# Moving the sums of an output stage from GpSimd to VectorE in a fused decoder layer

## The chip, the cores and the metric

The kernel runs on one core of a Trainium2 chip. The time of a run is the device time in microseconds (us). The engines have names in the profile: PE is TensorE (its weight loads are PEld), DVE is VectorE, ACT is ScalarE, POOL is GpSimd, and SP starts transfers.

## What is computed

One decoder layer over 1024 tokens of width 1024, all in float32: a SwiGLU feed-forward, a mixer, a second feed-forward, and a last RMSNorm. Around each of the three there is a norm before it and a gated residual behind it.

```python
mod = jax.nn.silu(c) @ ada_w[l] + ada_b[l]
sh1, sc1, gt1, sh2, sc2, gt2, sh3, sc3, gt3 = jnp.split(mod, 9, axis=-1)
u = modulate(rmsnorm(h, norm1_w[l]), sh1, sc1)
h = h + 0.5 * gt1[:, None, :] * swiglu(u, ffn1_w_in[l], ffn1_w_out[l])
u = modulate(rmsnorm(h, norm2_w[l]), sh2, sc2)
...                                  # mixer: sparse attention and retention, merged into `mixed`
h = h + gt2[:, None, :] * (mixed @ w_out[l])
u = modulate(rmsnorm(h, norm3_w[l]), sh3, sc3)
h = h + 0.5 * gt3[:, None, :] * swiglu(u, ffn2_w_in[l], ffn2_w_out[l])
return rmsnorm(h, final_norm_w)
```

The three products that end in `h + ...` are the output products: two with a contraction of 2816 (the feed-forwards) and one with a contraction of 1024 (`mixed @ w_out`). They are what the change is about.

## The kernel before, in words

`h` is kept transposed in eight tiles `hT[d]` of 128 features by 1024 tokens; `hf` is the half of the tokens (512 each). Every float32 product is made of three products of a faster type: each operand is split into a high part (ScalarE, a rounding copy) and a low part (VectorE, the difference to the original), and TensorE adds high by high, high by low and low by high.

The output products run in `out_seven`. It uses a Strassen-Winograd scheme: a 2 by 2 block product is made of seven block products `q` instead of eight, at the price of sums of blocks before and after. The contraction is walked in chunks of pairs of row blocks, (4, 3, 4) pairs in the feed-forwards and one chunk of 4 pairs in the projection (`single`). For each chunk and each `q` there are four PSUM tiles `po[d]` and, for each pair `k`, twelve matmuls of 128x128 by 128x512.

- `ops(c, k, q)` makes the operands. For `q` of 5, 7 and 6 it sums blocks of the weights on the engine `left` (`s1`, `s3`, `s2`; L659, L663, L668) and blocks of the gated product on `right`, VectorE (L660, L665, L670). Then ScalarE copies the high parts (L678) and VectorE makes the low parts (L679) of two operands into a tile `wp`, of which there are four. After 2 or 6 it makes two more sums (L683 on VectorE, L685).
- `post` takes a finished `po[d]`: for `q` of 2, 3 and 4 the residual, on VectorE (`residual`, L789, which multiplies by the gate and adds to `hT`), and for the others a copy into an accumulator by ScalarE (L706). In the last chunk of a feed-forward a sum of two accumulators stands behind `q` = 1 (L708).
- `between` makes further sums of accumulators in the last chunk (L716 to L726), and one more residual. Before `q` with an accumulator, ScalarE copies the accumulator into `po` (L751).
- `squares` prepares the next norm: ScalarE squares a half tile of `hT` (L194 for the first of a half, L197 else, into a temporary of which there are two for each half), and a sum adds it to `sqacc` (L198). `rstd_cols` then reduces `sqacc` over partitions on TensorE (L207) and takes a root on ScalarE (L210) and a reciprocal on VectorE (L211).

In `finish` (the last norm) ScalarE and GpSimd scale `hT` (L1274, L1276), TensorE transposes (L1284), and VectorE and ScalarE write the output rows (L1290, L1288). GpSimd has other work of its own near these stages: the gated merge before the projection (L1241), and the low parts of one pair of weights of the second feed-forward (L261).

The order of the instructions on each engine isn't written out by hand: a planner puts them in order from the program's order and its own estimate of their times, with some parts marked as urgent. Each engine works through its queue in that order; an instruction that waits holds up those behind it.

Of the kernel before, what the change touches and what calls it, by code (L numbers as in the profile page):

```python
# [48 lines left out]
def f32(ap):  # L49
    return ap.bitcast(F32)  # L50


class Layer:
# [135 lines left out]
    def squares(self, d, hf, pool, state, i):  # L189
        nc = self.nc  # L190
        h = self.hT[d][:, hf * H2:(hf + 1) * H2]
        if hf not in state:
            state[hf] = pool.tile([P, H2], F32, name="sqacc", bufs=2)
            nc.scalar.activation(state[hf], h, AF.Square)  # L194
        else:
            q = self.tmp.tile([P, H2], F32, name="t2" if hf else "t1", bufs=2)
            nc.scalar.activation(q, h, AF.Square)  # L197
            (nc.vector if (i != 2 and d == 3 if hf else d > 3) else nc.gpsimd).tensor_add(state[hf], state[hf], q)  # L198

    def rstd_cols(self, hf, pool, sums, state):  # L200

# [393 lines left out]
    def out_seven(self, i, chunks, wsrc, gsrc, free, acc, state, then, have=None):  # L595
# [3 lines left out]
        nc = self.nc  # L599
        single = len(chunks) == 1  # L600
# [4 lines left out]
        chunks = prs  # L605
# [45 lines left out]
        def ops(c, k, q):  # L651

            g = lambda n: have[c, k, n][1]
            drop = lambda n: free.append(have.pop((c, k, n)))
            ren = lambda a, b: have.__setitem__((c, k, b), have.pop((c, k, a)))
            left = nc.vector if single and q == 7 else nc.gpsimd
            right = nc.vector
            if q == 5:
                left.tensor_add(g("s1"), g("b1"), g("b2"))  # L659
                right.tensor_sub(g("b11"), g("b12"), g("b11"))  # L660
                ren("b11", "t1")
            elif q == 7:
                left.tensor_sub(g("b1"), g("a1"), g("b1"))  # L663
                ren("b1", "s3")
                right.tensor_sub(g("b12"), g("b22"), g("b12"))  # L665
                ren("b12", "t3")
            elif q == 6:
                left.tensor_sub(g("s1"), g("s1"), g("a1"))  # L668
                ren("s1", "s2")
                right.tensor_sub(g("t1"), g("b22"), g("t1"))  # L670
                ren("t1", "t2")
                drop("a1")
            n = {1: ("a1", "b11"), 2: ("a2", "b21"), 3: ("s4", "b22"), 4: ("b2", "t4"), 5: ("s1", "t1"),
                 6: ("s2", "t2"), 7: ("s3", "t3")}[q]
            w = self.W.tile([P, 2, 2, H2], F32R, name="wp", bufs=self.wb)
            res = []
            for x in range(2):
                nc.scalar.copy(w[:, x, 0], g(n[x]))  # L678
                nc.vector.tensor_sub(w[:, x, 1], g(n[x]), f32(w[:, x, 0]))  # L679
                res.append((w[:, x, 0], w[:, x, 1]))  # L680
            done.append((c, k, q))
            if q in (2, 6) and (c, k, 8 - q) in done:
                right.tensor_sub(g("b21"), g("b21"), g("t2"))  # L683
                ren("b21", "t4")
                (nc.vector if single else left).tensor_sub(g("a2"), g("a2"), g("s2"))  # L685
                ren("a2", "s4")
                drop("s2")
                drop("t2")
            if q in (3, 4, 7):
                for x in n:  # L690
                    drop(x)
            return res

        def res(r, hf, d, x, end=False):
            self.residual(i, 4 * r + d, hf, x)
            if end:
                self.squares(4 * r + d, hf, self.normp, state, i)
# [3 lines left out]
        def post(q, d, p, c, last):  # L701
            A = {x: acc[x][d] for x in acc}
            if q in (2, 3, 4):
                res(q == 4, q == 3, d, p, last)
                return
            nc.scalar.copy(A[1 if q == 6 and single else q], p)  # L706
            if last and q == 1 and not single:
                nc.gpsimd.tensor_add(A[6], A[6], A[1])  # L708

        def between(q):  # L710

            for d in range(4):
                A = {x: acc[x][d] for x in acc}
                if single:
                    if q == 2:
                        nc.gpsimd.tensor_add(A[1], A[1], A[7])  # L716
                        nc.gpsimd.tensor_sub(A[7], A[5], A[7])
                    elif q == 6:
                        nc.gpsimd.tensor_add(A[5], A[5], A[1])
                        res(1, 1, d, A[5])  # L720
                        nc.gpsimd.tensor_add(A[7], A[7], A[1])
                elif q == 6:
                    nc.gpsimd.tensor_add(A[7], A[7], A[6])
                elif q == 4:
                    nc.gpsimd.tensor_add(A[6], A[6], A[5])
                    nc.gpsimd.tensor_add(A[7], A[7], A[5])  # L726
                    res(1, 1, d, A[7])

        fetch()
        for c, prs in enumerate(chunks):  # L730
            last = c == len(chunks) - 1
            m = len(prs)
            for j, q in enumerate((1, 2, 5, 7, 6, 4, 3) if not last else (1, 5, 7, 2, 6, 4, 3) if single else
# [18 lines left out]
                if last and (q == 2 if single else q == 4):  # L752
                    between(q)
# [6 lines left out]
                if q == 3 and last and m <= self.wb:  # L760
                    xs = [ops(c, k, q) for k in range(m)]
                    for d in range(4):
                        for k in range(m):
                            mm(d, k, *xs[k])
                        post(q, d, po[d], c, last)
                        next(then, None)
                        next(then, None)
                    continue
                for k in range(m):
                    x = ops(c, k, q)  # L770
                    fetch()
                    for d in range(4):
                        mm(d, k, *x)
                for d in range(4):
                    post(q, d, po[d], c, last)
                if last and q == 6:
                    between(q)
# [821 lines left out]
```

## Time and profile before

| | us |
|---|---|
| median of 3 runs | 2420.77 |
| lowest and highest | 2418.34, 2423.05 |
| the profiled execution | 2416.41 |
| its span, first to last instruction | 2414.6 |
| TensorE busy in it | 2268.8 |
| VectorE busy | 1814.4 |
| ScalarE busy | 1055.3 |
| GpSimd busy | 1220.1 |

The profile shows one execution. Its rows give for a group of instructions the engine, the line of the kernel, the operation, the tile written and the tiles read, their shape, and how many there are. Idle time before an instruction is put down to the instruction that ended it. Busy time of TensorE is modelled, since matmuls are pipelined; the count of matmuls is the safer number.

### The profile page before, as it was taken

What the parts mean: (1) busy time and instruction counts of PE and PEld (TensorE: products, weight loads), DVE (VectorE), ACT (ScalarE), POOL (GpSimd) and SP (SyncE); (2) the same over time, 40 slices, a digit from 0 to 9 for tenths busy, and PEclk for the clock granted to TensorE, in tenths of its full rate; (3) what the DMA queues carried; (4) which work ended last, traced back from release to release, by engine and by line L of the source; (5) the groups of instructions that cost most, each with busy time, mean ns of one, the idle gap of its engine ahead of it and who ended that gap; (6) DMA issues with size and microseconds to landing.
All of it is one profiled execution on the core that took longest, in us unless ns stands there. A gap on an engine that the chain in (4) does not pass through costs nothing.

```text
span 2414.6 us, 32683 instructions
## 1 busy us (share of the span) xinstructions
PE 2268.8 (94%) x11563; PEld 1903.5 (79%) x11563; DVE 1814.4 (75%) x2742; ACT 1055.3 (44%) x1904; POOL 1220.1 (51%) x900
## 2 busy tenths in 40 slices
PE   7799999999997999999997999999889999999997
PEld 5578888878876899887876889877668888887886
DVE  7888888578999855677667887759885555558987
ACT  5432222235764322123347776725432222225675
POOL 3856354544476544464315544456754444436447
PEclk9999999999998999999998999999889999999998
DMA  9135656263204344343552121460322222245301
GB/s 349 58 102 170 208 168 200 90 236 131 88 1 135 92 139 129 101 144 117 158 154 80 62 88 62 162 214 1 105 64 84 79 82 80 79 164 208 103 17 70
DMA packets 248888, 288.32 MB, mean 119 GB/s; under 512 B 14852, under 2 KB 169236, under 8 KB 248724
## 3 DMA queue, kind: packets, MB, share of 16 engines
q1 hardware_dynamic: 248608, 286.19, 37.2%
q8 instruction: 91, 1.49, 0.3%
q14 instruction: 73, 0.60, 0.1%
q10 hardware_dynamic: 116, 0.05, 0.0%
HBM read 216.45 MB, written 69.73 MB: 119 GB/s over the span
## 4 chain that ended last, share of the span: by engine, by line
PE 32%; DVE 9%; DMA 3%; ACT 3%; issue 2%; POOL 1%; SPq 0%; DVEq 0%; ACTq 0%; POOLq 0%
PE po L281 17%; DVE wp L679 3%; PE s L758 3%; PE po L758 3%; PE ot L1173 2%; PE pt L1159 2%; PE s L281 2%; PE s L1071 1%; DMA tn<-d_gab 1%; DVE hT L789 1%; PE s L1070 1%; DMA hT<-d_h 1%; PE pt L862 1%; PE ot L1170 0%; PE po L495 0%
## 5 line engine op out<-in xcount | busy, mean ns | idle before, releaser
L281 PE MATMUL po<-u0h,wp 128*128 128x512 f32 x944 | 305.3, 395 | 7.3 <-DVE gates L998 4.9
L758 PE MATMUL po<-wp 128*128 128x512 f32 x1128 | 271.8, 397 | 17.1 <-DVE wp L679 16.3
L281 PE MATMUL po<-u1h,wp 128*128 128x512 f32 x880 | 282.0, 391 | 3.5 <-DVE bias L544 2.2
L758 PEld LDWEIGHTS po<-wp 128*128 128x128 f32 x1128 | 214.6, 192 | 70.5 <-DVE wp L679 24.7
L758 PE MATMUL s<-wp 128*128 128x512 f32 x1056 | 252.5, 395 | 15.6 <-DVE wp L679 15.0
L758 PEld LDWEIGHTS s<-wp 128*128 128x128 f32 x1056 | 199.8, 190 | 62.8 <-DVE wp L679 20.5
L334 ACT CAST wp<-S 128x1024 fp32r<-128x1024 f32 x98 | 103.0, 1051 | 307.1 <-PE po L281 303.1
L281 PEld LDWEIGHTS po<-u0h,wp 128*128 128x128 f32 x944 | 179.5, 190 | 46.1 <-DVE gates L998 5.1
L463 POOL TENSOR_TENSOR t<-t,t 128x512 f32<-128x512 f32 x38 | 56.3, 1482 | 303.0 <-DVE t L407 193.7
L281 PEld LDWEIGHTS po<-u1h,wp 128*128 128x128 f32 x880 | 165.1, 188 | 40.3 <-DVE bias L544 2.6
L281 PE MATMUL po<-u0l,wp 128*128 128x512 f32 x472 | 186.1, 394 | 0.0
L281 PE MATMUL po<-u1l,wp 128*128 128x512 f32 x440 | 172.5, 392 | 2.5 <-DVE u1l L243 2.5
L335 DVE TENSOR_TENSOR wp<-S,wp 128x1024 fp32r<-128x1024 f32 x98 | 158.7, 1619 | 16.1 <-ACT wp L334 15.9
L334 ACT CAST wp<-raw 128x1024 fp32r<-128x1024 f32 x98 | 82.0, 837 | 185.7 <-PE po L281 174.1
L341 POOL TENSOR_TENSOR S<-raw 128x512 f32<-128x512 f32 x49 | 68.9, 1406 | 155.1 <-DMA raw<-w_in 47.6
L281 PE MATMUL po<-t2h,wp 128*128 128x512 f32 x392 | 132.2, 397 | 3.0 <-ACT t2h L300 3.0
L281 PE MATMUL po<-t4h,wp 128*128 128x512 f32 x392 | 131.5, 396 | 1.1 <-DVE tn L399 1.1
L281 PE MATMUL po<-t3h,wp 128*128 128x512 f32 x392 | 132.0, 397 | 0.2 <-DVE t L395 0.2
L335 DVE TENSOR_TENSOR wp<-raw,wp 128x1024 fp32r<-128x1024 f32 x98 | 113.0, 1154 | 12.0 <-ACT wp L334 11.8
L395 DVE TENSOR_TENSOR t<-tn,po 128x512 f32<-128x512 f32 x57 | 39.1, 685 | 110.3 <-issue 78.5
L1163 DVE TENSOR_TENSOR pl<-pt,ph 128x512 fp32r<-128x512 f32 (+2 forms) x160 | 97.0, 619 | 13.8 <-ACT ph L1162 13.0
L281 PEld LDWEIGHTS po<-u0l,wp 128*128 128x128 f32 x472 | 90.0, 191 | 18.3
(467 smaller groups left out, 6195.2 us busy)
## 6 DMA issues: line engine op xcount, KB each, us to landing
raw<-ffn_w_in SPq DMA_DIRECT2D x88, 512.0 KB, 4.7
raw<-ada_w SPq DMA_DIRECT2D x56, 512.0 KB, 4.5
raw<-w_in SPq DMA_DIRECT2D x40, 512.0 KB, 4.1
d_g<-t SPq DMA_DIRECT2D x50, 256.0 KB, 2.0
d_h<-hT SPq DMA_DIRECT2D x24, 512.0 KB, 4.7
hT<-d_h SPq DMA_DIRECT2D x48, 256.0 KB, 5.3
d_g<-tg SPq DMA_DIRECT2D x38, 256.0 KB, 2.0
fw<-ada_w SPq DMA_DIRECT2D x8, 1024.0 KB, 11.0
```

The source lines that it names most:

```text
L281: nc.tensor.matmul(ps, a, b, start=k == 0 and q == 0, stop=k == n - 1 and q == 2)
L334: nc.scalar.copy(w[:, 0], t)
L335: nc.vector.tensor_sub(w[:, 1], t, f32(w[:, 0]))
L341: nc.gpsimd.tensor_add(s[:, 0:4], b[:, 0:4], b[:, 4:8])
L395: nc.vector.tensor_add(c, u2, p)
L463: nc.gpsimd.tensor_mul(g, g, t)
L679: nc.vector.tensor_sub(w[:, x, 1], g(n[x]), f32(w[:, x, 0]))
L758: nc.tensor.matmul(po[d], l[:, e], r, start=k == 0 and z == 0 and not seeded, stop=k == m - 1 and z == 2, skip_group_check=seeded)
L789: self.nc.vector.scalar_tensor_tensor(h, po, self.ab[:, 3 * i + 2, d:d + 1], h, op0=ALU.mult, op1=ALU.add)
L1159: nc.tensor.transpose(pt[:, o + j * P:o + (j + 1) * P], a, self.ident)
L1163: nc.vector.tensor_sub(lo, pt[:, :n], f32(hi))
L1173: nc.tensor.matmul(ot, self.V2[kt // 4][:, kt % 4, b, g, :], x[:, o:o + 2 * P], start=first and m == 0, stop=last and m == 1)
```

## The change

All sums of the last chunk of the output products, and all sums of squares, are made on VectorE. In earlier chunks of the feed-forwards `left` stays GpSimd. In the projection the one chunk is also the last.

```diff
         else:
             q = self.tmp.tile([P, H2], F32, name="t2" if hf else "t1", bufs=2)
             nc.scalar.activation(q, h, AF.Square)
-            (nc.vector if (i != 2 and d == 3 if hf else d > 3) else nc.gpsimd).tensor_add(state[hf], state[hf], q)
+            nc.vector.tensor_add(state[hf], state[hf], q)
...
-            left = nc.vector if single and q == 7 else nc.gpsimd
+            left = nc.vector if c == len(chunks) - 1 else nc.gpsimd
...
-                (nc.vector if single else left).tensor_sub(g("a2"), g("a2"), g("s2"))
+                left.tensor_sub(g("a2"), g("a2"), g("s2"))
...
             if last and q == 1 and not single:
-                nc.gpsimd.tensor_add(A[6], A[6], A[1])
+                nc.vector.tensor_add(A[6], A[6], A[1])
...
                 if single:
                     if q == 2:
-                        nc.gpsimd.tensor_add(A[1], A[1], A[7])
-                        nc.gpsimd.tensor_sub(A[7], A[5], A[7])
+                        nc.vector.tensor_add(A[1], A[1], A[7])
+                        nc.vector.tensor_sub(A[7], A[5], A[7])
                     elif q == 6:
-                        nc.gpsimd.tensor_add(A[5], A[5], A[1])
+                        nc.vector.tensor_add(A[5], A[5], A[1])
                         res(1, 1, d, A[5])
-                        nc.gpsimd.tensor_add(A[7], A[7], A[1])
+                        nc.vector.tensor_add(A[7], A[7], A[1])
                 elif q == 6:
-                    nc.gpsimd.tensor_add(A[7], A[7], A[6])
+                    nc.vector.tensor_add(A[7], A[7], A[6])
                 elif q == 4:
-                    nc.gpsimd.tensor_add(A[6], A[6], A[5])
-                    nc.gpsimd.tensor_add(A[7], A[7], A[5])
+                    nc.vector.tensor_add(A[6], A[6], A[5])
+                    nc.vector.tensor_add(A[7], A[7], A[5])
                     res(1, 1, d, A[7])
```

## Rows read from the trace of the kernel before

**Rows 1.** The page, part 1: busy time, share of the span, instructions.
```profile
PE 2268.8 (94%) x11563; PEld 1903.5 (79%) x11563; DVE 1814.4 (75%) x2742; ACT 1055.3 (44%) x1904; POOL 1220.1 (51%) x900
```
**Rows 2.** Windows: stretch, length; busy us and instructions; granted clock, DMA share, GB/s.
```profile
580.00:632.00 52.00, 51.85 (x229) 42.64 (x228) 48.56 (x58) 35.50 (x66) 24.27 (x14) 1.00 0.26 82
655.40:689.60 34.20, 33.97 (x151) 27.80 (x150) 28.82 (x35) 26.59 (x51) 18.40 (x8) 1.00 0.00 1
689.60:731.20 41.60, 35.70 (x140) 27.23 (x138) 41.46 (x34) 24.58 (x44) 36.37 (x22) 0.92 0.00 0
1619.10:1640.40 21.30, 14.71 (x53) 10.09 (x51) 21.30 (x21) 9.41 (x17) 15.29 (x10) 0.92 0.00 1
1655.40:1706.80 51.40, 45.11 (x185) 34.96 (x183) 50.59 (x45) 30.96 (x54) 37.49 (x24) 0.97 0.10 41
2345.10:2390.70 45.60, 40.17 (x162) 31.64 (x160) 45.46 (x41) 28.62 (x51) 43.03 (x28) 0.93 0.00 1
```
**Rows 3.** Timeline, TensorE's weight loads: start, duration, engine, line, what, count.
```profile
1642.47 10.84 PEld L758 LDWEIGHTS s<-wp 128*128 128x128 f32 x48
```
**Rows 4.** Windows of 5 us, and TensorE's timeline (idle before, releaser in brackets).
```profile
715.00:720.00 5.00, 1.20 (x6) 0.66 (x4) 5.00 (x5) 3.19 (x7) 5.00 (x4) 0.99 0.00 0
720.00:725.00 5.00, 4.06 (x10) 3.19 (x11) 5.00 (x4) 3.81 (x6) 5.00 (x4) 0.50 0.01 3
...
720.94 4.63 PE L758 MATMUL s<-wp 128*128 128x512 f32 x10 [4.74 <-DVE wp L679]
```
**Rows 5.** Timeline, VectorE in a stretch without GpSimd.
```profile
647.49 0.69 DVE L660 TENSOR_TENSOR u0l<-u0l 128x512 f32<-128x512 f32 x1
648.09 0.68 DVE L679 TENSOR_TENSOR wp<-u0l,wp 128x512 fp32r<-128x512 f32 x1
```
**Rows 6.** Timeline, VectorE and GpSimd side by side.
```profile
669.58 1.77 DVE L679 TENSOR_TENSOR wp<-u1l,wp 128x512 fp32r<-128x512 f32 x1
671.28 1.78 DVE L679 TENSOR_TENSOR wp<-u0l,wp 128x512 fp32r<-128x512 f32 x1
...
669.07 3.43 POOL L708 TENSOR_TENSOR acc<-acc,acc 128x512 f32<-128x512 f32 x2
```
**Rows 7.** The line of the sums of squares: count, shortest/median/longest ns, first and last start.
```profile
L198 POOL TENSOR_TENSOR sqacc<-sqacc,t x28: 1264/1616/2243, 718.6 to 2399.0; 128x512 f32<-128x512 f32 x28
...
L198 DVE TENSOR_TENSOR sqacc<-sqacc,t x14: 678/692/2477, 734.9 to 2392.4; 128x512 f32<-128x512 f32 x14
```
**Rows 8.** GpSimd's groups by line, in 1619.1:1640.4, 1655.4:1706.8, 2345.1:2390.7, one each.
```profile
L1241 POOL TENSOR_TENSOR mix<-tn,ga 128x512 f32<-128x512 f32 x2 | 3.4, 1703 | 2.0 <-DVE tn L1240 2.0
...
L261 POOL TENSOR_TENSOR wp<-raw,wp 128x1024 fp32r<-128x1024 f32 x2 | 5.2, 2609 | 5.6 <-ACT wp L260 5.6
...
L1276 POOL TENSOR_SCALAR hT<-hT,cols 128x512 f32<-128x512 f32 x6 | 8.4, 1403 | 0.0
```
**Rows 9.** Timeline behind the first feed-forward, GpSimd and ScalarE.
```profile
739.45 4.28 POOL L198 TENSOR_TENSOR sqacc<-sqacc,t 128x512 f32<-128x512 f32 x3 [9.45 <-ACT t L197]
...
740.76 0.63 ACT L197 ACTIVATE t<-hT 128x512 f32<-128x512 f32 x1 [0.73 <-POOL sqacc L198]
741.29 0.25 ACT L210 ACTIVATE rstd<-s,eps 128x4 f32<-128x4 f32 x1
```
**Rows 10.** Timeline behind the second feed-forward, GpSimd and TensorE.
```profile
2394.90 5.33 POOL L198 TENSOR_TENSOR sqacc<-sqacc,t 128x512 f32<-128x512 f32 x4 [0.97 <-ACT t L197]
...
2403.95 0.24 PE L207 MATMUL s<-ones,sqacc 128*128 128x1 f32 x1 [0.32 <-DVE raw L1290]
```
**Rows 11.** Timeline, GpSimd's first L668 of the last chunk.
```profile
657.51 6.50 POOL L668 TENSOR_TENSOR u1l<-u1l,u0l 128x512 f32<-128x512 f32 x1 [25.68 <-DVE wp L679]
```
**Rows 12.** Windows behind the first feed-forward and behind the projection.
```profile
745.00:800.00 55.00, 44.09 (x247) 39.51 (x248) 52.19 (x58) 22.66 (x37) 40.18 (x26) 0.86 0.32 94
...
1790.00:2155.00 365.00, 365.00 (x1587) 297.75 (x1586) 195.56 (x212) 104.46 (x133) 167.25 (x112) 1.00 0.27 84
```
**Rows 13.** Waits from 2310 to 2416 us: who for whom, us in total, times, longest.
```profile
ACT t L197 <- DVE sqacc L198: 5.1, 2, 2.7
```

## The prediction

> **What bounds the kernel now.** I read the page first: TensorE is busy for 94% of the span [rows 1], so a change beside it can only win where TensorE stands still. Next I looked for the lines of the diff (the chain of waits, the order in time, the idle time of TensorE) and found that they run in three places: the last chunk of the first feed-forward (585 to 745 us), the output projection (1595 to 1715 us) and the last chunk of the second feed-forward (2240 to 2400 us). Then I cut these into stretches [rows 2]. In the early ones, 580 to 632 and 655.4 to 689.6, TensorE is busy to within 0.3 us of the whole, so nothing can be won there. In the four late ones VectorE is busy for all but 1.1 us of 159.9 (41.46 of 41.6, 21.30 of 21.3, 50.59 of 51.4, 45.46 of 45.6) while TensorE has gaps. A chain of 48 weight loads takes 10.84 us, 0.226 us each [rows 3], so the 140, 53, 185 and 162 matmuls of these stretches need 31.6, 12.0, 41.8 and 36.6 us: 122 of 159.9. VectorE is the bound there, and one gap shows what it costs: TensorE waits 4.74 us for a VectorE split (L679), its clock is granted at 0.50 in the next 5 us (1.2 of 2.4 GHz), and ten matmuls take 4.63 us [rows 4].
>
> Why is VectorE full? Alone, its 128x512 sums and splits take 0.68 us each and start 0.60 us apart [rows 5]. Beside back-to-back GpSimd sums of the same shape they take 1.77 us and start 1.70 us apart, exactly in step with GpSimd's own 1.7 us [rows 6]. The two engines take turns. Check over whole stretches: 34 instructions x 0.605 = 20.6 us, but VectorE is busy 41.46; the 20.9 us on top, over 22 GpSimd instructions, is 0.95 us each. The same sum gives 0.86 (1619 to 1640, 10 of them), 0.97 (1655 to 1707, 24 of them) and 0.74 (2345 to 2391, 28 of them). So a sum on GpSimd costs VectorE about 0.95 us there, and on VectorE itself it would cost 0.605.
>
> **The change, part by part.** It moves 116 instructions and nothing else; none issues a DMA. Per feed-forward: 16 sums of weights (L659, L663, L668, L685) and 16 of accumulators (L708, L723, L725, L726). In the output projection: 8 (L659, L668) and 16 (L716, L717, L719, L721). And the 28 sums of squares that GpSimd makes; 14 are on VectorE already [rows 7].
>
> Late stretches. Of GpSimd's instructions, 2, 2 and 6 stay (L1241, L261, L1276) [rows 8]; 22, 8, 22 and 22 move.
> - 689.6 to 731.2: 56 x 0.605 + 0.5 (eight residuals that read PSUM, 0.06 each) = 34.4 us; now 41.6: 7.2 won.
> - 1619.1 to 1640.4: 29 x 0.605 + 2 x 0.86 for those that stay = 19.3; now 21.3: 2.0 won.
> - 1655.4 to 1706.8: 67 x 0.605 + 0.5 + 2 x 0.95 = 42.9; now 51.4: 8.5 won. TensorE needs 41.8 there, so nearly all that can be had.
> - 2345.1 to 2390.7: 63 x 0.605 + 0.7 = 38.8, plus what the six L1276 cost. They read one tensor; 28 x 0.74 = 20.7 is what 22 x 0.95 gives alone, so their price lies between 0 and 0.7 us each; I take the middle, 2 us: 40.8; now 45.6: 4.8 won.
> Sum 22.5 us. All four stay above TensorE's needs, but only just: two engines that are both nearly full won't mesh without gaps. In the early stretch after 655, where TensorE is full, VectorE is idle for 5.4 of 34.2 us [rows 2]; in the late ones now for under 1%. I take 5% of the new 137.4 us, 6.9 us, as lost, between these and nearer to the late ones, since VectorE stays the bound; bounds 0 and 16%.
>
> Ends. After the first feed-forward, ScalarE's squares wait for GpSimd's adds (three in 4.28 us), and the root of the first half's sums stands behind these squares [rows 9]. Three adds of 0.605 us take 1.8, 2.5 less; I take 2 us as won (0 to 2.5). After the second, four adds on GpSimd end at 2400.2, but the matmul that reads them starts only at 2403.95, after other work [rows 10]: 0.5 us (0 to 2). After the projection I take 0: the last three stretch VectorE by about what they then cost on it.
>
> Early parts: 16 moved sums per feed-forward. Most are paired as in rows 6; a few cost VectorE nothing now (the one at 657.51 waits 6.50 us while VectorE keeps its pace [rows 11]) and will cost 0.6. At most 16 x 0.605 = 9.7 us more; the cover is VectorE's idle 3.4 and 5.4 us [rows 2] and the stretching that goes. Cost 0; without the cover up to 1 us a stage.
>
> New waits: a sum of accumulators (L708, L719) waits for ScalarE's copy, and now the splits behind it on VectorE's queue wait too, and TensorE for these. The trace before doesn't show it; a copy lasts about 0.6 us, some eight groups, so 0 to 5 us, part of the 5%. What is late next is TensorE itself. The gain passes on: behind the first feed-forward VectorE is busy for 52.19 of 55 us, and behind the projection's norm TensorE for 365.00 of 365 [rows 12], so an earlier start there is an earlier end.
>
> Total: 22.5 + 2.5 - 6.9 = 18 us. The profiled execution took 2416.4 us (span 2414.6 and 1.8 around it), 4.4 under the median of the runs shown, 2420.8. So 2398.4 against the former, 2402.8 against the latter; I predict 2403.
>
> **The rivals.** (a) Only part is won: the order in which VectorE takes the moved sums puts them ahead of splits that TensorE needs. The gap loss is then 16% (22 us) instead of 5%: 3 us won, 2418; between, 2408 to 2418. For it: the gap of rows 4 is already one in which a split came late behind other work. Against: the GpSimd sums now hold up the same queue.
> (b) Slower: ScalarE stands behind the sums of squares. A square (L197) needs one of two buffers, freed by the add two before it; ScalarE's casts (L678) queue behind it, and VectorE's splits behind these. Where the add is on VectorE already, such waits last 2.4 to 2.7 us [rows 13]. Three of them in each of three stages, uncovered, cost 24 us against 18: 2427. It decides once VectorE has four or more instructions (2.4 us) ahead of each add. Against: ScalarE is busy for only 94 of the 159.9 us of the late stretches [rows 2], and adds on GpSimd make it wait as well [rows 9].
> (c) Slower by far: VectorE is stretched by something else than GpSimd, and the 74 moved instructions come on top: 74 x 0.605 = 45 us on a full engine, 2466. Rows 5 and 6 speak against it: same lines, same shapes, 0.68 or 1.77 us by whether GpSimd works. The Trainium skill, Perfetto Trace Analysis, section Optimizing Scalar/DVE Operations, is on this rival's side in one sentence: where VectorE is saturated, giving some work to ScalarE or even GpSimd may make sense; its next one says that between VectorE and GpSimd this might not help, since they share a read port. By the first the change would cost this rival's time; the trace agrees with the second.
> (d) Nothing arrives: each stage ends earlier, but the next waits for something of its own, 2416 to 2421. Against: rows 12.
> (e) No gaps at all and L1276 free: 22.5 + 2 + 5 = 29.5 won, 2391.
>
> **How the numbers follow.** Forecast (10 to 25 us won, 2396 to 2411): 0.64. (e) and what lies towards it, 0.07; (a) 0.14; (d) 0.06; (b) 0.07; (c) 0.02. The range takes in the forecast, most of (a) and of (e): 2390 to 2418. Faster by over 0.2% (4.8 us, about what a measurement of this kernel can tell from no change): 0.64 + 0.07 + 0.09 of (a) = 0.80. Slower: (b), (c) = 0.09. The rest, 0.11, is the same.
>
> **What would show it.** In the profile after, L679 should be near 0.69 us in these stages, its median now mixed with 1.78; GpSimd should have nothing in them but L1241, L261 and L1276; the 4.74 us gap and the granted clock of 0.50 behind it should go; TensorE's busy share in the late stretches should rise from 85% to above 90%; 2.0 + 8.5 us should be won in the projection, the largest part. Wrong would make it: waits of L197 for VectorE's L198 (b), L679 at 1.7 us with GpSimd idle (c), TensorE waiting for L679 as long as now (a).

## The result and the profile after

Before: 2419.8 us median (2418.3 to 2423.1; one run more than above). After: 2395.5 us median (2390.5 to 2396.2). The ratio is 0.989, with an interval of 0.988 to 0.991: 24 us faster. The profiled execution took 2396.2 us (span 2394.4), its span 20.2 us less than that of before.

The page of the kernel after, part 1 (answers [rows 1]):

```profile
PE 2263.2 (95%) x11563; PEld 1904.2 (80%) x11563; DVE 1774.0 (74%) x2858; ACT 1054.5 (44%) x1904; POOL 1025.2 (43%) x784
```

VectorE makes 116 instructions more and is busy for 40.4 us less: what GpSimd's sums had cost it was more than the sums themselves.

Windows of the kernel after (answers [rows 2]; columns as there). The stretches from the third to the sixth hold the same weight loads (give or take one) as the matching stretches of before, so that their lengths can be compared:

```profile
655.40:689.60 34.20, 34.20 (x153) 28.32 (x152) 26.85 (x44) 26.98 (x52) 0.00 (x0) 1.00 0.00 1
689.60:731.20 41.60, 40.60 (x178) 33.08 (x177) 39.30 (x65) 27.59 (x50) 0.00 (x0) 1.00 0.13 51
691.90:732.20 40.30, 39.23 (x171) 31.61 (x169) 38.78 (x64) 26.21 (x48) 0.00 (x0) 1.00 0.13 53
1616.60:1650.00 33.40, 30.09 (x120) 24.00 (x119) 31.34 (x50) 20.70 (x39) 2.40 (x2) 0.90 0.00 1
1650.00:1693.70 43.70, 42.07 (x185) 34.16 (x183) 40.29 (x67) 31.32 (x56) 6.36 (x2) 1.00 0.12 49
2332.70:2369.50 36.80, 36.34 (x161) 29.81 (x160) 36.80 (x60) 27.21 (x49) 10.42 (x5) 1.00 0.00 1
```

Two windows of the kernel before for this comparison that [rows 2] doesn't hold; the first counts L758's instructions alone (TensorE and its weight loads), the second those of all engines:

```profile
689.60:738.60 49.00, 43.03 (x171) 32.97 (x169) 0.93 0.11 43
...
1619.10:1655.40 36.30, 29.59 (x119) 22.42 (x118) 34.19 (x41) 20.61 (x39) 17.62 (x11) 0.95 0.00 0
```

For 169 loads 40.3 us instead of 49.0; for 119 (118) 33.4 instead of 36.3; for 183 43.7 instead of 51.4; for 160, 36.8 instead of 45.6 [rows 2]. TensorE is now busy for 97% of the first of them, 96% of the third and 99% of the fourth. GpSimd does nothing in the first feed-forward's last chunk. L679 there and in the projection is at 0.68 us; its median for the projection's operands was 1.22 before:

```profile
L679 DVE TENSOR_TENSOR wp<-mix,wp x28: 677/682/1797, 1594.8 to 1687.2; 128x512 fp32r<-128x512 f32 x28
```

The columns of this line are the shortest, median and longest ns, and the first and last start.

The ends of the stages got worse. TensorE and VectorE behind the first feed-forward, and two windows (answers [rows 9] and [rows 4]):

```profile
737.20 1.87 PE L207 MATMUL s<-ones,sqacc 128*128 128x1 f32 x8 [5.07 <-DVE sqacc L198]
...
732.08 2.06 DVE L789 SCALAR_TENSOR_TENSOR hT<-po,ab,hT 128x512 f32<-128x512 f32 x3
734.06 3.09 DVE L198 TENSOR_TENSOR sqacc<-sqacc,t 128x512 f32<-128x512 f32 x5
...
735.00:740.00 5.00, 1.87 (x8) 1.78 (x8) 4.80 (x8) 3.91 (x7) 0.00 (x0) 0.71 1.08 362
740.00:745.00 5.00, 3.68 (x10) 2.21 (x10) 2.23 (x5) 0.32 (x2) 0.00 (x0) 0.50 1.09 334
```

The last L758 ends at 732.1, but L207 of the first half must wait until 737.2 for the sums of squares, which stand in VectorE's queue in turn with those of the second half, behind the residuals; the granted clock is 0.50 in the 5 us from 740 (1.2 of 2.4 GHz). Behind the projection the same wait lasts 5.50 us.

Where the time went, by the same instructions in the profiled executions (us for each part; the kernels of the later columns are the experiments below). For L758 the end of the last one counts, for the others the start. L815 and L998 are the first products behind the first feed-forward and the last copy of their results, L1240 is the gating ahead of the projection, L495 the first products of a feed-forward. Each column is one execution, and the runs of one kernel lie 2 to 12 us apart, so a difference of 1 or 2 us in a part says little.

| part, from the end of the one before | before | after | e1 | m1 | i1 | a1 | a2 |
|---|---|---|---|---|---|---|---|
| to the first L668 | 531.4 | 533.8 | 531.4 | 531.6 | 532.1 | 533.1 | 532.9 |
| to the last L758, first feed-forward | 207.1 | 198.3 | 198.7 | 199.0 | 197.3 | 192.4 | 192.6 |
| to the last L998 | 59.8 | 62.3 | 60.0 | 59.9 | 68.1 | 63.1 | 60.0 |
| to the first L1240 (mixer) | 772.8 | 773.3 | 777.8 | 775.3 | 767.7 | 775.4 | 774.3 |
| to the last L758, projection | 135.9 | 125.9 | 126.8 | 125.4 | 125.3 | 125.7 | 128.6 |
| to the last L495 | 36.7 | 39.4 | 37.8 | 37.6 | 36.8 | 38.6 | 38.5 |
| to the last L659 | 539.7 | 539.7 | 540.3 | 540.4 | 544.4 | 533.2 | 534.0 |
| to the last L758, second feed-forward | 109.4 | 98.9 | 99.3 | 99.2 | 99.6 | 100.7 | 101.1 |
| to the end | 21.8 | 22.8 | 26.9 | 24.6 | 20.8 | 22.9 | 21.1 |

Before to after: 8.8 + 10.0 + 10.5 = 29.3 us won up to the last L758 of the three stages, 2.5 + 2.7 + 1.0 = 6.2 lost at their ends, 2.4 lost ahead of the first L668 and 0.5 in the mixer, where nothing was changed (e1, whose code is the same up to there, has no loss ahead of L668). Sum 20.2.

### The profile page after: what moved, and what is told of

Same layout as the page of the kernel before. It is cut to its first block, busy times and chain, and to the rows that moved or that the text cites. A ratio compares the mean times of both kernels' runs of the same rounds, so it can differ in the third digit from the quotient of the medians.

```text
span 2394.4 us, 32603 instructions
## 1 busy us (share of the span) xinstructions
PE 2263.2 (95%) x11563; PEld 1904.2 (80%) x11563; DVE 1774.0 (74%) x2858; ACT 1054.5 (44%) x1904; POOL 1025.2 (43%) x784
## 3 DMA queue, kind: packets, MB, share of 16 engines
q1 hardware_dynamic: 248608, 286.19, 37.6%
## 4 chain that ended last, share of the span: by engine, by line
PE 37%; DVE 6%; DMA 3%; ACT 2%; issue 1%; POOL 1%; SPq 0%; DVEq 0%; ACTq 0%; POOLq 0%
PE po L281 17%; PE po L758 5%; PE s L758 5%; PE ot L1173 3%; PE pt L1159 2%; PE s L281 2%; PE s L1070 1%; PE s L1071 1%; DMA tn<-d_gab 1%; DVE wp L679 1%; PE pt L862 1%; PE ot L1170 0%; POOL mix L1241 0%; POOL tg L251 0%; DVE pl L1163 0%
## 5 line engine op out<-in xcount | busy, mean ns | idle before, releaser
L758 PE MATMUL po<-wp 128*128 128x512 f32 x1128 | 268.7, 394 | 10.5 <-DVE wp L679 7.8
L758 PEld LDWEIGHTS po<-wp 128*128 128x128 f32 x1128 | 214.2, 190 | 59.3 <-DVE wp L679 10.5
L758 PE MATMUL s<-wp 128*128 128x512 f32 x1056 | 249.1, 392 | 4.1 <-DVE wp L679 2.5
L758 PEld LDWEIGHTS s<-wp 128*128 128x128 f32 x1056 | 199.1, 189 | 47.3 <-DVE wp L679 4.0
L251 POOL TENSOR_SCALAR tg<-tn,mod 128x512 f32<-128x512 f32 x32 | 36.6, 1149 | 160.6 <-DVE tn L240 151.5
```

The lines of the kernel that those rows point to most:

```text
L251: nc.gpsimd.tensor_scalar(t2, t, b, 1.0, op0=ALU.add, op1=ALU.mult)
L758: nc.tensor.matmul(po[d], l[:, e], r, start=k == 0 and z == 0 and not seeded, stop=k == m - 1 and z == 2, skip_group_check=seeded)
```

## The experiments

Theory T: VectorE and GpSimd take turns, so GpSimd's sums cost a full VectorE more than they would cost on it. Rivals: the moved sums of squares are the gain; VectorE is stretched by something else (c). Later ones came from the traces.

**One part alone.** e1 moves the sums of weights and accumulators only, e2 the sums of squares only.

```diff
# e1, against the changed kernel
-            nc.vector.tensor_add(state[hf], state[hf], q)
+            (nc.vector if (i != 2 and d == 3 if hf else d > 3) else nc.gpsimd).tensor_add(state[hf], state[hf], q)
# e2: this line alone the other way round, in the kernel before
```

> Moves the sums of weight blocks and of accumulators to VectorE (88 of the 116 instructions) and leaves the 28 sums of squares on GpSimd. Theory T (a GpSimd sum beside a full VectorE costs it 0.95 us; since almost all of the moved sums in the late stretches are of this kind, they hold nearly all of the gain; what the changed kernel then gave back, it gave back in the sums of squares at the ends of the first feed-forward and of the projection, about 5 us each, where TensorE's L207 waits 5.07 and 5.50 us for VectorE's L198): the last L758 of the first feed-forward ends near 733 us and the first L815 near 742, the whole 5 to 10 us faster than the changed kernel, 2386 to 2391. As predicted on record (ends win 2.5 us, no loss there): 2 to 5 us slower than the changed kernel, 2398 to 2400. Rival (the gain is that of the sums of squares): 2415 to 2420.

> The other part alone: only the 28 sums of squares move to VectorE; all sums of weights and accumulators stay on GpSimd. Theory T: in the late stretches hardly any of them run, so L679 stays near 1.7 us there and the last L758 of each stage ends within 3 us of the kernel before; at the ends TensorE waits for L198 on VectorE: 2417 to 2425, the same or slightly slower than before. As predicted on record: 2 to 3 us faster than before, 2417. Rival (the gain is theirs): 2395 to 2400.

e1: 2399.3 us, ratio 0.991 (0.989 to 0.993), 22 us won. e2: 2415.2, ratio 0.997 (0.996 to 0.999), 6 us won. The sums of weights and accumulators hold most of the gain; the rival falls. The prediction's numbers (2398 to 2400, 2417) were nearer than theory T with its loss at the ends. In e1's trace that loss is gone where it was expected (first L815 at 738.2 instead of 746.7), but the lead didn't last. TensorE of e1, and two windows:

```profile
1119.84 0.71 PE L928 MATMUL pi<-qT,kT 64*128 64x128 f32 x6 [1.72 <-ACT kT L922]
...
1120.00:1125.00 5.00, 5.00 (x33) 4.42 (x34) 3.24 (x9) 1.43 (x3) 3.96 (x4) 0.64 0.40 91
1125.00:1130.00 5.00, 5.00 (x16) 3.89 (x16) 2.39 (x7) 0.37 (x1) 0.62 (x1) 0.68 0.26 93
```

The same place in the kernel after:

```profile
1122.87 0.71 PE L928 MATMUL pi<-qT,kT 64*128 64x128 f32 x6 [0.55 <-ACT kT L922]
...
1125.00:1130.00 5.00, 5.00 (x32) 4.14 (x32) 3.46 (x11) 0.37 (x1) 2.07 (x4) 1.00 0.65 184
```

Far from every changed line, in the mixer, e1's TensorE stands for 1.72 us instead of 0.55, and the clock is granted at 0.64 and 0.68 behind it instead of 1.00. By the starts of the same ScalarE instructions, e1's lead over the kernel before falls from 7.7 to 3.4 us over this stretch, while the changed kernel's stays at 3.4; e1's whole mixer took 777.8 us, the changed kernel's 773.3. Another 4 us went in the last norm (26.9 instead of 22.8), where GpSimd's sums of squares come late. e2's profiled execution (2420.9) was the longest of its runs, so its trace doesn't place the 6 us; it has the long gap ahead of L928 as well (1.74 us).

**The price of a GpSimd instruction.** e3 and e4 add GpSimd work beside the changed kernel, of two inputs and of one.

```diff
+            if c == len(chunks) - 1:
+                nc.gpsimd.tensor_add(self.spare, f32(w[:, 0, 1]), f32(w[:, 1, 1]))          # e3
+                nc.gpsimd.tensor_scalar(self.spare, f32(w[:, 0, 1]), 2.0, None, op0=ALU.mult)  # e4
             done.append((c, k, q))
```

> The changed kernel, and in each of the 28 steps of each last chunk GpSimd also adds the low parts of the two operands into a tile that nobody reads (84 additional instructions, 128x512, two inputs). VectorE's own work is that of the changed kernel. Theory T (taking turns, 0.95 us each where VectorE is full; VectorE's slack in the last chunk of the first feed-forward is 34.2 + 41.6 - 26.85 - 39.30 = 9.7 us): 28 x 0.95 - 9.7 = 17 us lost per stage, up to 51 in all; 20 to 51 slower than the changed kernel, 2415 to 2447, with L679 at 1.5 us or more wherever GpSimd adds. Rival c (VectorE is stretched by something else than GpSimd): within 3 us of the changed kernel, 2393 to 2399, L679 at 0.68.

> As the run before, but GpSimd multiplies one low part by a constant instead of adding two (84 instructions of one input, 128x512, behind the same waits). Theory T with what L1276 shows in the changed kernel (two of them stretch to 7.68 us while VectorE keeps its pace at 0.68): VectorE isn't stretched, within 3 us of the changed kernel, 2393 to 2399. If any work of GpSimd on the same memory costs VectorE turns: as the run before, 2415 or more. If the cost of the run before comes from the waits on the buffers and not from the turns: both slow by the same.

e3: 2449.5 us, ratio 1.011 (1.009 to 1.013), 54 us above the changed kernel, somewhat more than theory T's upper end (2447). e4: 2417.8, ratio 0.998 (0.997 to 1.000), 22 above it: neither free, as theory T had it, nor the price of e3. VectorE and GpSimd in e3 (its lines are shifted: L680 is L679, L683 the added sum):

```profile
700.74 0.68 DVE L688 TENSOR_TENSOR u1h<-u1h,u0h 128x512 f32<-128x512 f32 x1
701.34 1.80 DVE L686 TENSOR_TENSOR u0h<-u0h,u0l 128x512 f32<-128x512 f32 x1
703.07 0.68 DVE L680 TENSOR_TENSOR wp<-u1h,wp 128x512 fp32r<-128x512 f32 x1
...
700.96 1.63 POOL L683 TENSOR_TENSOR spare<-wp 128x512 f32<-128x512 f32 x1 [1.90 <-DVE wp L680]
```

One VectorE instruction is stretched by 1.12 us for one GpSimd sum, and the next is at 0.68 again. Rival (c) falls: VectorE's own work is the same, and only GpSimd was added.

e4 has two costs in one: turns, and the `wp` buffers that a late GpSimd instruction holds. TensorE's waits for L758 (L761) by releaser, in us and times, in e4:

```profile
  DVE wp L680: 21.1, 24
  ACT wp L679: 16.8, 10
```

ScalarE's casts, for which the changed kernel waits 2.5 us, now hold TensorE up for 16.8. So e5 and e6 do the same with a constant tile as input, released by a ScalarE copy of one column; no operand buffer is held.

```diff
+    def beside(self, low): x = next(self.mark); m = self.marks[:, x:x + 1]; self.nc.scalar.copy(m, f32(low)); ...
+        self.nc.gpsimd.tensor_scalar(self.spare, self.ident[:, None, :].to_broadcast([P, 4, P]), m, None, op0=ALU.mult)   # e5
+        self.nc.gpsimd.tensor_mul(self.spare, self.ident[:, None, :].to_broadcast([P, 4, P]), m[:, :, None].to_broadcast([P, 4, P]))   # e6
```

> The changed kernel with 84 GpSimd multiplications of one input (128x512) beside it, as e4_one_input_beside, but they read a constant tile instead of the operands: they hold no wp buffer, and are released by a ScalarE copy of one column (128x1) behind the cast of each step. In e4 the 84 instructions cost 22 us, VectorE was stretched by some 0.4 us in about every second one, and TensorE stood 16.8 us before ScalarE's casts (ACT wp), which the changed kernel doesn't show. Theory B (what e4 cost is mostly the held buffers): 2396 to 2404. Rival (it is the turns on VectorE: 84 x 0.25 = 21 us): 2413 to 2420.

> As e5_one_input_free, but each of the 84 GpSimd instructions has two inputs (the constant tile by the column). Theory T (turns: e3's trace shows 1.1 us on one VectorE instruction for nearly each GpSimd sum): 84 x 0.95 = 80 us at most, less VectorE's slack of about 10 us a stage: 2430 to 2447, with TensorE waiting for L679 and not for ScalarE's casts. If what e3 cost was mostly held buffers: under 2410.

e5: 2404.0 us, ratio 0.995 (0.994 to 0.997), 8.5 above the changed kernel by the medians and 14 by the ratios. e6: 2435.8, ratio 1.007 (1.005 to 1.009), 40 by the medians and 43 by the ratios. e6 lies in theory T's range, e5 at the upper edge of theory B's. The waits for casts are gone (0.5 and 1.4 us). Now the last chunk of the first feed-forward, in before, after, e3, e4, e5 and e6, one fence each. Behind the window and its length stand TensorE, its weight loads, VectorE (third pair), ScalarE and GpSimd (fifth pair), each with busy us and count:

```profile
655.00:738.60 83.60, 77.46 (x324) 61.50 (x324) 77.77 (x80) 54.12 (x99) 54.77 (x30) 0.96 0.07 26
```
```profile
655.00:732.20 77.20, 76.13 (x334) 62.16 (x332) 67.55 (x111) 55.58 (x104) 0.00 (x0) 1.00 0.07 28
```
```profile
655.00:742.50 87.50, 76.18 (x319) 58.73 (x318) 85.18 (x109) 54.50 (x101) 61.96 (x24) 1.00 0.06 25
```
```profile
655.00:737.00 82.00, 77.76 (x323) 61.81 (x321) 70.84 (x108) 54.09 (x101) 68.68 (x25) 0.96 0.07 26
```
```profile
655.00:731.50 76.50, 72.23 (x312) 57.89 (x311) 68.48 (x105) 54.98 (x119) 73.67 (x24) 1.00 0.07 28
```
```profile
655.00:741.20 86.20, 79.12 (x318) 62.20 (x316) 85.06 (x110) 57.98 (x126) 49.84 (x24) 0.92 0.06 25
```

Without GpSimd a VectorE instruction takes 67.55 / 111 = 0.61 us here. What is busy beyond that, divided by GpSimd's instructions, is what each costs VectorE: before (77.77 - 80 x 0.61) / 30 = 0.97 us; e3 0.78, e6 0.75; e4 0.20, e5 0.18. The two-input price is the same with and without held buffers. A one-input instruction costs a quarter of it. What e4 lost beyond e5, 8 to 14 us, is put down to the held buffers: VectorE's price is the same in both, and the waits for casts are in e4 (and e3, 21.0 us), not in e5 and e6.

**The order at the ends.** m1 makes the squares by stage (as before in the first two, on VectorE in the last). i1 keeps the changed kernel's engines and pins the second half's squares behind the first half's. c1 takes m1's engines and pins in the last stage alone.

```diff
# m1
-            nc.vector.tensor_add(state[hf], state[hf], q)
+            (nc.vector if i == 2 or (d == 3 if hf else d > 3) else nc.gpsimd).tensor_add(state[hf], state[hf], q)
# i1 (c1: m1's engine, and "i == 2 and hf and d > 3")
+            sq = nc.scalar.activation(q, h, AF.Square)
+            for x in [sq, nc.vector.tensor_add(state[hf], state[hf], q)]: (self.tc.keep_in_program_order(x) if hf and d > 3 else None)
```

> The sums of weights and accumulators on VectorE as in the changed kernel; the sums of squares as in the kernel before for the first feed-forward and the projection, and all on VectorE for the second feed-forward. In e1 (all squares as before) the first L815 came 8.5 us earlier than in the changed kernel, but the end of the second feed-forward took 26.9 us from the last L758, against 22.8 in the changed kernel. Theory E (each stage end stands for itself): the end as in the changed kernel, 4 us less than e1: 2391 to 2396, less if the 8 us that e1 had won at 1100 us aren't lost behind the 1.72 us gap at 1118 us. Rival (an order that differs in one place shifts everything behind it, and e1's longer end is of that kind): as e1, 2397 to 2402.

> The changed kernel, with the squares and sums of squares of rows 4 to 7 of the second half pinned behind those of the first half on ScalarE and VectorE; no instruction is added or moved to another engine. Theory S (in the changed kernel the first half's sums stand behind the second half's in VectorE's queue, and TensorE's L207 waits 5.07 and 5.50 us for them at the ends of the first feed-forward and the projection): L207 starts within 1 us of the last L758, the first L815 comes about 5 us earlier, and the whole is 5 to 10 us faster than the changed kernel: 2386 to 2391. Rival (the second half comes later by as much, and the stages behind wait for it, or the gain is lost behind the gap at 1118 us as in e1): 2394 to 2400.

> The changed kernel with the sums of squares of the first feed-forward and the projection as in the kernel before (as m1_squares_by_stage), and in the second feed-forward the second half's pinned behind the first half's (as i1_first_half_first, where the end took 120.4 us from the last L659 against 123.8 in m1 and 121.7 in the changed kernel). Theory E (each stage end stands for itself): 3 us less than m1: 2388 to 2391. Rival (what is won at one end is lost behind it): 2392 to 2396, as the changed kernel.

m1: 2392.8 us (2388.3 to 2395.1), ratio 0.989. i1: 2392.5 (2391.0 to 2393.7), ratio 0.990. c1: 2392.0 (2388.1 to 2393.1), ratio 0.988 (0.986 to 0.990). All three are about 3 us below the changed kernel's median, but by the ratios, which compare each with the kernel before in the same session, m1 (0.989) and i1 (0.990) are where the changed kernel is (0.989), and all three intervals overlap its own. m1 lies in theory E's range, though its end took 24.6 us and not 22.8. TensorE in i1, then the matching place of its last rows in the kernel after:

```profile
730.09 1.05 PE L207 MATMUL s<-ones,sqacc 128*128 128x1 f32 x8 [0.74 <-DVE sqacc L198]
...
737.99 2.23 PE L815 MATMUL po<-wp,u0h 128*128 128x280 f32 x8 [4.36 <-ACT u0h L246]
...
750.24 0.78 PE L815 MATMUL po<-wp,u0l 128*128 128x280 f32 x4 [2.49 <-DVE u0l L248]
...
1765.59 0.79 PE L281 MATMUL po<-t2h,wp 128*128 128x512 f32 x1 [7.21 <-ACT t2h L300]
...
1773.02 0.80 PE L281 MATMUL po<-t3l,wp 128*128 128x512 f32 x1 [2.38 <-DVE t3l L301]
...
1775.91 0.79 PE L281 MATMUL po<-t2l,wp 128*128 128x512 f32 x1 [1.67 <-DVE t2l L301]
```
```profile
1765.55 0.50 PE L281 MATMUL po<-t2h,wp 128*128 128x512 f32 x1 [1.42 <-ACT t2h L300]
1774.72 0.80 PE L281 MATMUL po<-t2l,wp 128*128 128x512 f32 x1 [8.67 <-DVE t2l L301]
```

The wait of 5.07 us is 0.74, and the first L815 comes at 738.0 instead of 746.7: the order was the cause of that wait. But the whole gained 3 us at most, not 5 to 10. What the first half wins the second pays: VectorE has the second half's sums in between the products of the norm (wait of 2.49 us for L248), and the last L998 comes at 797.4 instead of 794.4.

In the second feed-forward TensorE waits for the splits of sums of the normed input (L300, L301), 11.3 us in three gaps in i1 and 10.1 us in two in the changed kernel, with VectorE busy without a pause from 1760 to 1775 us in both; the granted clock in the three windows of 5 us from 1765 to 1780 is 0.50 each time in i1, and 0.79, 0.50 and 0.68 in the changed kernel. By the starts of the same weight loads i1 is 5.6 us ahead just before this place, and only 0.6 us ahead after it.

i1's 2392.5 us lies between its two forecasts; what the trace shows is the rival's mechanism. c1 decides nothing: by the median it is where its rival has it, by the ratios 3 us under m1, as theory E has it.

**The same idea further.** a1 moves the weight sums of the earlier chunks as well; a2 adds c1's order.

```diff
-            left = nc.vector if c == len(chunks) - 1 else nc.gpsimd
+            left = nc.vector
```

> The changed kernel, with the weight sums on VectorE in the first two chunks of both feed-forwards too (56 more instructions moved; GpSimd then makes no sums of the output products at all). Theory T: in the first chunk of the first feed-forward the changed kernel still shows the old picture (VectorE busy for 29.54 of the 30 us from 530 to 560, eight of its instructions stretched to 1.77, TensorE idle for 4.5 us and its clock at 0.89); the second feed-forward shows the same at 2170 to 2200. Moving these sums wins about 5 us in each: 2384 to 2388. As the prediction on record had it (where TensorE is full, sums of GpSimd are hidden): no change, 2393 to 2398. Rival c (the moved instructions come on top): 56 x 0.6 = up to 20 us slower.

> a1_all_chunks and c1_both_orders together. If the gains add: 2379 to 2385. If they don't: as the better of the two, 2384 to 2391.

a1: 2385.8 us (2384.5 to 2386.9), ratio 0.986 (0.983 to 0.988), in theory T's range; its interval just overlaps the changed kernel's. a2: 2384.3 (2380.2 to 2385.2), ratio 0.985 (0.983 to 0.987), faster than before and than the changed kernel, whose own interval lies above 0.9875. The first chunk of the first feed-forward, in the kernel after and in a1:

```profile
530.00:560.00 30.00, 25.48 (x104) 20.16 (x103) 29.54 (x37) 12.17 (x22) 21.33 (x10) 0.94 0.32 114
```
```profile
530.00:560.00 30.00, 30.00 (x134) 24.86 (x133) 29.44 (x49) 15.53 (x29) 0.00 (x0) 1.00 0.62 203
```

Thirty more matmuls in the same 30 us, and twelve more VectorE instructions in the same busy time: theory T's picture holds outside the changed stretches as well. The parts of the table show 198.3 to 192.4 and 539.7 to 533.2, 12.4 us together; 9.7 arrive in the medians. a1 too has the wait at 1119 (1.73 us, clock 0.57 and 0.74 behind it), a2 hasn't. The gains of a1 and c1 didn't add up in a way that these runs can tell from a1 alone.

## Why the prediction came out right

The forecast was 18 us won (2403.0), the result 24 by the medians and 20.2 by the profiled executions, inside the forecast's own 10 to 25. The mechanism was right; the size was right by luck in part, because two terms were off in opposite directions: the stretches with their loss for meshing (22.5 - 6.9 forecast, 29.3 measured to the last matmuls) and the ends (2.5 forecast, -6.2 measured).

- **VectorE is the bound, and it is full because of GpSimd's turns: right.** 0.95 us per sum was read from [rows 2] and [rows 5, 6]; the last chunk as a whole gives 0.97, and GpSimd sums put back cost 0.75 to 0.78. Each is above the 0.61 that a sum costs on VectorE, which is the whole case for the change. Of the two sentences that the prediction took from the Trainium skill, Perfetto Trace Analysis, section Optimizing Scalar/DVE Operations, this case goes against the first (offload a saturated VectorE): the kernel before, which does so with GpSimd, takes 24 us longer. It bears out the second; e3 and e6 show the price of sharing, 54 and 40 us.
- **The sum of the late stretches: too small where it was far off, in the second feed-forward.** Forecast 7.2, 2.0, 8.5 and 4.8; by equal weight loads 8.7 (in a stretch longer by 7 us, to the last matmul), 2.9 (in one longer by 15 us), 7.7 and 8.8. The 4.8 had 2 us in it for six L1276. They cost VectorE nearly nothing: five of them stretched to 10.42 us, where six had taken 8.4 [rows 8], while VectorE made 60 instructions in 36.80 us, 0.61 each. The lower bound, 0, was the right end; the value taken was the middle.
- **The 5% for meshing, 6.9 us: wrong.** By the 0.226 us of [rows 3] the loads need 38.2, 26.9, 41.4 and 36.2 us; the stretches took 40.3, 33.4, 43.7 and 36.8. In three of them TensorE's needs are met within 0.6 to 2.3 us, even where VectorE has no pause at all (36.80 of 36.80 us in the last); the last took less than the 38.8 that the prediction had for VectorE without L1276. VectorE works ahead: in 655.4 to 689.6, where [rows 2] has 35 instructions in 28.82 us, it makes 44 in 26.85. Only the first stretch of the projection takes 6.5 us more than its loads need.
- **Early parts at 0: right,** by the same row; nine more instructions, 2 us less busy. (The sum at 657.51 of [rows 11] is 6.50 us long; what it waited is the 25.68 in brackets.) That also tells why a1 wins: the prediction looked at 580 to 632 and 655 to 690, where TensorE is full, and not at 530 to 560, where it isn't.
- **The ends, +2.5 us: wrong in sign,** -6.2 us. The step counted the duration of three adds (4.28 us on GpSimd, 1.8 on VectorE) and not their place: on GpSimd the second half's sums had a queue of their own, on VectorE they alternate with the first half's. Who waits behind a moved instruction had been asked for splits, not for the sums among themselves. That L207's wait came from this order is shown by i1. Since i1 is 3 us faster at most, the order alone doesn't account for the loss; that two halves of a norm on one full engine are the rest is likely but not shown, since m1, whose squares in these two places are back on GpSimd, is no faster than i1.
- **The gain passes on: right for the projection** (539.7 us from its norm to the last L659 in both), right for the first feed-forward in the changed kernel (772.8 and 773.3 us in the mixer), and in part only in e1 and a1, where a longer gap at 1119 us and the lower clock behind it took back 4.3 and 4.5 us. This can't be read from the trace of before.
- **Rivals.** (b): the waits of L197 came (4.3, 5.0 and 1.5 us at the three ends; [rows 13] had 5.1 in the last), but at the ends, where no operand's cast stood behind them. (c) fell in e3. (d) shows in small, at the ends. (e), no gaps and L1276 free, was nearest to what the stretches did; its 2391 was missed because of the ends. Of the signs named, L679's median in the projection (`mix`) went from 1.22 to 0.68 us, the 4.74 us gap is gone, and the projection won 10.0 to its last matmul for the 2.0 + 8.5 forecast.

What stays open: which of the two engines gets the turn (below), where e2's 6 us lie, and why the gap at 1119 us is long in some kernels.

## What to carry to other kernels

Before an engine is relieved, compare what a neighbour's instruction costs it (here 0.75 to 0.97 us) with what the instruction would cost on it (0.61): divide the stretched engine's excess busy time by the neighbour's count, over a whole stretch. Price moved work by its place in the queue too, above all where two chains that had an engine each now share one. A gain at a stage's end can be lost in the next stage where the same engine is full (i1: 5.6 us ahead, then 0.6); here three other orders of the ends gave 3 us at most, while the same change in two more chunks gave 10.

## What the runs showed of the hardware

**Either engine can be the one that waits.** GpSimd, then VectorE, in the first chunk of the kernel after:

```profile
545.37 1.60 POOL L685 TENSOR_TENSOR u0l<-u0l,u1h 128x512 f32<-128x512 f32 x1
550.36 9.51 POOL L668 TENSOR_TENSOR u1h<-u1h,u0h 128x512 f32<-128x512 f32 x1 [3.39 <-DVE wp L679]
...
555.02 2.48 DVE L679 TENSOR_TENSOR wp<-u1h,wp 128x512 fp32r<-128x512 f32 x4
557.43 0.68 DVE L679 TENSOR_TENSOR wp<-raw,wp 128x512 fp32r<-128x512 f32 x1
558.03 0.68 DVE L679 TENSOR_TENSOR wp<-u0h,wp 128x512 fp32r<-128x512 f32 x1
559.17 1.25 DVE L679 TENSOR_TENSOR wp<-raw,wp 128x512 fp32r<-128x512 f32 x1 [0.46 <-ACT wp L678]
```

A sum of 1.6 us takes 9.51 while VectorE goes on at 0.60 us a piece, and ends at 559.87, right behind VectorE's first pause, of 0.46 us; the VectorE instruction behind the pause then takes 1.25. In [rows 6] each VectorE instruction is held up instead. The Trainium skill, SBUF — State Buffer, section SBUF: two separate sides, says of two such instructions that whichever starts first keeps the shared ports for its whole length, and the other is fully blocked. The rows agree with that. Which engine is next when both have more to do, these runs don't settle.

**One input is cheap for VectorE, but not for GpSimd.** In e5 24 multiplications of one input are busy for 73.67 us, 3.1 each, where the shortest of the 84 takes 1.56. In the changed kernel two of L1276, 0.69 us alone, take 7.68 us beside a full VectorE. VectorE pays 0.18 us for each in e5.

**The clock as a second price of a gap.** A gap of 0.55 us ahead of L928 (after) was followed by a granted clock of 1.00, gaps of 1.72 and 1.73 us (e1, a1) by 0.64 and 0.57. TensorE of e2, and the 5 us behind it:

```profile
1126.43 0.71 PE L928 MATMUL pi<-qT,kT 64*128 64x128 f32 x6 [1.74 <-ACT kT L922]
...
1126.50:1131.50 5.00, 5.00 (x33) 4.42 (x34) 3.21 (x9) 1.51 (x3) 4.06 (x4) 0.64 0.39 90
```

Coming earlier isn't what makes the gap long: e2 comes to this place when the kernel before does (1126.3, gap 0.53 us) and has it, a2 comes there 12.6 us earlier and has 0.69 us. The traces don't show the cause; one execution of each kernel was traced.
